# A two-layer decoder trunk on one core: the tensor engine's products of each attention issued in source order

## The chip, the cores and the metric

The kernel runs on one core of a Trainium2 chip. The metric is the device time of one execution in microseconds (us). The profile is that of one further execution; its span is the time between its first and its last recorded instruction.

## The reference, cut to what matters

256 tokens of width 1024 pass through two layers. The first attends with 16 heads of 64 to its own keys and values (at this length the block-sparse selection leaves the causal block of 256 alone); the second attends, in a sliding window of 128 with one learned sink per head, to four shared key and value heads. Each layer ends in a gated feed-forward part of width 2816 with a causal convolution of width 3.

```python
for l in range(DEPTH):                       # DEPTH = 2
    h = rmsnorm(x, attn_norm[l])
    if l < N_A:                              # layer 0
        q, k, v = jnp.split(h @ w_qkv_a[l], 3, axis=-1)
        o = moba_attention(rope(q), rope(k), v)
    else:                                    # layer 1, keys and values shared
        k, v = jnp.split(rmsnorm(x, kv_norm) @ w_kv_b, 2, axis=-1)
        o = swa_sink_attention(rope(h @ w_q_b[i]), rope(k), v, sinks_b[i])
    x = x + o @ w_o
    x = x + conv_ffn(rmsnorm(x, ffn_norm[l]), w_up[l], conv_w[l], conv_b[l], w_down[l])
return rmsnorm(x, final_norm)
```

## The kernel before, in words

All products keep float32 accuracy by splitting each operand into a rounded part ("hi") and the rest ("lo"); each product is three: hi with hi, hi with lo, lo with hi. The weights stream from memory in 90 units of 128 x 2048 (`wr`). For each, ScalarE (ACT) writes the hi part (`wh`, line 179) and VectorE (DVE) the lo part (`wl`, line 184), each in two or four pieces; both engines do this all through the program, a few units ahead of the TensorE (PE).

An attention (`attention`, line 408) works on four groups of four heads. For a group g:

- `scores(g)` (line 423): six products with the keys laid out in blocks (lines 432 to 434, into a bank `sd`), then twelve products that use half of the array's rows (line 439), two at a time, one for each of two banks `u`. Their operands are the queries and keys turned to feature order by `to_feature` (line 384): four transposes (line 388), a hi copy on ACT (line 399), a lo difference on DVE (line 394). The first four of the twelve need the hi part alone; the next two need the lo part.
- the softmax of each head (line 444): DVE masks the scores and takes their extreme (line 456), ACT takes the exponential (line 464), then DVE forms the reciprocal (line 469) and scales the first third of the row (line 476) while ACT scales the rest (line 474).
- `probs_T` (line 483): three transposes per head (line 489) into a bank `u`, of which the first reads what DVE scaled and the other two what ACT scaled; a copy out of the bank by DVE (line 497) or ACT (line 495).
- `values(g)` (line 503): eight products that use half of the array's columns (line 512; 16 entries in the profile), whose result is split into hi (ACT, line 518) and lo (DVE, line 519).

Between these pieces `fill` draws full-size products from a `filler`: projections of later heads (`proj`, lines 347 to 349), and then the output projection (`Down.mm`, lines 558 to 561; the hi products first, line 561 last, which needs the lo part of line 519). `attention` is called twice, for layer 0 (line 938) and layer 1 (line 1004).

What sets the order: steps on ACT and DVE are put off by a clock that the kernel keeps while it is written out (`chain`, `tick`), and the framework's scheduler then orders each engine's instructions by its own estimate of when each is ready. Inside `tc.manual_schedule(engines=...)` the engines named keep the order in which the source issues them. Before, this holds for PE, ACT, DVE and SP from the start to line 524 in layer 0 (`manual.close()`) and for ACT and DVE in the tail (line 1048); within the loop over the groups, PE's order is the scheduler's. In the trace each engine's instructions begin in the order in which they stand in the program, so that one that waits holds those behind it.

Of the kernel before, what the change touches and what calls it, by code (L numbers as in the profile page):

```python
# [60 lines left out]
def trunk(ctx: ExitStack, tc, x, xw, pos, cpk, fin, sinks, w, out):  # L61
# [20 lines left out]
    def quad(dt=F32R, name="q"):  # L82
        return spaced(qd, 4 * S, dt, "q", nm(name), 15).rearrange("p (c t) -> p c t", c=4)
# [4 lines left out]
    def row3(n=3 * P, edges=False):  # L88

        t = wk.tile([P, 3 * P + 8], F32, tag="m3", name=nm("m3"), bufs=8)  # L90
        return (t[:, 3:3 * P + 5], t[:, 4:3 * P + 4]) if edges else t[:, 4:4 + n]

    def bank(tag):
        return ps.tile([P, 512], F32, tag=tag, name=nm(tag), bufs=4 if tag == "acc" else 2)

    def f(ap):
        return ap.bitcast(F32)

    def blk(b):
        return slice(b * P, (b + 1) * P)  # L100
# [29 lines left out]
    def tick(ns):  # L130
        clock[0] += ns
        while put_off and not busy[0]:
            item = min(put_off, key=lambda t: t[0])
            if item[0] > clock[0]:
                return
            run_item(item)

    def chain(key, *steps, urgent=0):

        def run(k):  # L140
            if urgent:
                with tc.high_priority(offset=urgent):
                    steps[k][1]()
            else:
                steps[k][1]()
            if k + 1 < len(steps):
                put_off.append((clock[0] + steps[k + 1][0], key, lambda: run(k + 1)))
        put_off.append((clock[0] + steps[0][0], key, lambda: run(0)))

    def require(*key):  # L150

        while True:
            mine = [t for t in put_off if t[1] == key]
            if not mine:
                return
            run_item(min(mine, key=lambda t: t[0]))
# [251 lines left out]
    def attention(qk, ready, filler, lead, rate, msk, vcol, sink):  # L408
# [6 lines left out]
        def fill(ns):  # L415
            budget[0] += ns
            while budget[0] > 0:
                try:
                    budget[0] -= next(filler)
                except StopIteration:  # L420
                    return

        def scores(g):
            while g not in qk:
                next(filler)
            require("qk", g)
            qh, ql, kh_, kl_, kcol, diag = qk[g]
            sd, sa, sb = bank("t" if o_down[0].acc else "acc"), bank("u"), bank("u")
            for p in range(2):
                dh, dl = diag(p)  # L430
                o = sd[:, p * S:(p + 1) * S]
                nc.tensor.matmul(o, qh[:, p, blk(0)], dh, start=True, stop=False)
                nc.tensor.matmul(o, qh[:, p, blk(0)], dl, start=False, stop=False)
                nc.tensor.matmul(o, ql[:, p, blk(0)], dh, start=False, stop=True)
            for p in range(2):
                for k, (q_, k_) in enumerate(((qh, kh_), (qh, kl_), (ql, kh_))):
                    for e, o in enumerate((sa, sb)):
                        r = slice(e * HD, (e + 1) * HD)
                        nc.tensor.matmul(o[:, p * S:(p + 1) * S], q_[r, p, blk(1)], k_[r, kcol(p)],
                                         start=(k == 0), stop=(k == 2))  # L440
            tick(1600)
            return [softmax(2 * g + p, p, sd, (sa, sb)) for p in range(2)]
# [40 lines left out]
        def probs_T(j, pr):  # L483
            require("sm", j)
            out_ = []
            for e in range(2):
                tp = bank("u")
                for i in range(3):
                    nc.tensor.transpose(tp[:, i * P:(i + 1) * P], pr[e][:, i * P:(i + 1) * P], ident)  # L489
                tick(330)  # L490
                pT = row3()

                def copy(e=e, tp=tp, pT=pT):
                    if e:
                        nc.scalar.activation(pT, tp[:, :3 * P], AF.Copy)
                    else:
                        nc.vector.tensor_copy(pT, tp[:, :3 * P])

                chain(("pT", j), (200.0, copy))
                out_.append(pT)  # L500
            return out_

        def values(g, pT):

            ov = bank("t")
            for p in range(2):
                j = 2 * g + p
                require("pT", j)
                for kb in range(NB):
                    for e in range(2):  # L510
                        o = ov[e * HD:(e + 1) * HD, p * S:(p + 1) * S]
                        nc.tensor.matmul(o[:, P:] if kb else o, v_sb[kb][:, vcol(2 * j + e)],  # L512
                                         pT[p][e][:, S:] if kb else pT[p][e][:, :S], start=(kb == 0), stop=(kb == 1))
            tick(1600)
            q = quad()
            hi, lo = q[:, 0:2], q[:, 2:4]
            ov = ov.rearrange("p (j t) -> p j t", j=2)
            chain(("o", g), (200.0, lambda: nc.scalar.activation(hi, ov, AF.Copy)),
                  (600.0, lambda: nc.vector.tensor_tensor(out=lo, in0=ov, in1=f(hi), op=ALU.subtract)))
            oT.extend((hi[:, p], lo[:, p]) for p in range(2))  # L520
# [2 lines left out]
        fill(lead)  # L523
        manual.close()
        n_g = NH // 4
        state = scores(0)
        for g in range(n_g):
            pT = []
            for p in range(2):
                fill(rate(g)[p])  # L530
                pT.append(probs_T(2 * g + p, state[p]))
            fill(rate(g)[2])
            if g + 1 < n_g:
                state = scores(g + 1)
            values(g, pT)
        for _ in filler:
            pass
        return oT
# [396 lines left out]
    def ready_a(oT):  # L935
        o_down.append(Down(U_OA, 4, oT, lambda i: require("o", i)))

    attention(qk, ready_a, filler_a(), 8000.0, lambda g: (7000.0, 3500.0, 2000.0) if g < 3 else (4500.0, 2000.0, 1500.0), mask, lambda h: h, False)
    nc.gpsimd.affine_select(out=mask[:, :P], in_=mask[:, :P], compare_op=ALU.is_gt, fill=NEG, base=0,
                            pattern=[[1, P]], channel_multiplier=-1)  # L940
# [60 lines left out]
    def ready_b(oT):  # L1001
        o_down.append(Down(U_OB, 4, oT, lambda i: require("o", i)))

    attention(qk, ready_b, filler_b(), 2800.0, lambda g: (2700.0, 1400.0, 1000.0) if g else (3300.0, 1700.0, 1000.0), mask, lambda h: 2 * (h // 8) + h % 2, True)

    hT = new_hT()
# [149 lines left out]
```

## Time and profile before

| | us |
|---|---|
| median of 3 runs (lowest, highest) | 552.49 (552.43, 552.72) |
| the profiled execution | 551.98 |
| its span in the profile | 550.3 |
| PE busy | 542.5 |
| ACT busy | 372.8 |
| DVE busy | 419.9 |
| granted TensorE clock, mean | 0.998 |

1.7 us of the profiled execution lie around the span. "Busy" for PE is modelled: a product of 128 x 512 is shown with about 0.38 us, but the next one starts 0.22 us after it, so that the starts and not the durations tell what PE spends. The first attention's groups run from about 36 to 104 us of the span, the second's from about 316 to 360 us. In a row of the timeline stand the start, the time to the end of the last of the instructions merged in it, the engine, the source line, the operation, the output and inputs, the shape, and how many instructions are merged; in brackets the idle time ahead of it and what ended that.

### The profile page before, as it was taken

The page shows a single profiled execution, that of the slowest core. Times are in us where ns is not written, and L with a number is a line of the kernel's source. Part 1 is how long each engine was busy: PE and PEld are TensorE (multiplying, and loading weights), DVE is VectorE, ACT ScalarE, POOL GpSimd, SP SyncE. Part 2 cuts the span into 40 slices and gives each one's busy share as a digit, 9 for nine tenths or more (in the row PEclk, how much of TensorE's full clock was granted, in tenths as well). Part 3 has the DMA queues.
Part 4 walks back from the last instruction along what each step waited for, and adds up shares of the span by engine and source line. Part 5 has one row for each costly group of instructions (what it writes and reads, how often), then busy time and mean ns, then how long its engine had stood idle before and what let it go on. Part 6 is the DMA issues. An engine that isn't in the chain of part 4 may idle for free.

```text
span 550.3 us, 9930 instructions
## 1 busy us (share of the span) xinstructions
PE 542.5 (99%) x3762; PEld 497.7 (90%) x3762; DVE 419.9 (76%) x874; ACT 372.8 (68%) x726; POOL 113.3 (21%) x140
## 2 busy tenths in 40 slices
PE   8999999999999999999999999999999999999995
PEld 7888888899999999988888887889999999998884
DVE  6798778589798888865468789788898888884414
ACT  6998777678577777744448698877667777663313
POOL 7331001013322233220002000002532332210003
PEclk9999999999999999999999999999999999999999
DMA  8984335342555665565643524242465556665301
GB/s 322 384 302 166 142 153 191 116 155 78 200 212 205 227 230 206 186 232 219 208 174 154 198 109 154 78 152 77 154 249 211 210 195 213 248 224 215 114 0 76
DMA packets 15311, 100.98 MB, mean 184 GB/s; under 512 B 1952, under 2 KB 2080, under 8 KB 3744
## 3 DMA queue, kind: packets, MB, share of 16 engines
q1 hardware_dynamic: 14976, 100.09, 50.5%
q8 instruction: 29, 0.48, 0.3%
q10 hardware_dynamic: 288, 0.26, 0.1%
q14 instruction: 18, 0.15, 0.1%
HBM read 99.30 MB, written 1.05 MB: 182 GB/s over the span
## 4 chain that ended last, share of the span: by engine, by line
PE 97%; DMA 1%; issue 0%; POOL 0%; DVE 0%; DVEq 0%; POOLq 0%; ACT 0%
PE acc L558 10%; PE acc L559 9%; PE acc L561 9%; PE u L653 7%; PE u L651 7%; PE u L652 6%; PE t L653 6%; PE t L651 6%; PE t L652 6%; PE acc L347 5%; PE acc L349 5%; PE acc L348 5%; PE t L512 2%; PE u L489 2%; PE acc L765 2%; PE acc L653 2%
## 5 line engine op out<-in xcount | busy, mean ns | idle before, releaser
L184 DVE TENSOR_TENSOR wl<-wr,wh 128x1024 fp32r<-128x1024 f32 (+1 forms) x190 | 207.3, 1110 | 55.9 <-ACT wh L179 55.3
L179 ACT ACTIVATE wh<-wr 128x1024 fp32r<-128x1024 f32 (+1 forms) x190 | 176.4, 957 | 55.7 <-PE acc L561 44.6
L697 POOL TENSOR_TENSOR m<-m,m 128x256 f32<-128x256 f32 x44 | 70.6, 1605 | 166.7 <-DVE m L692 95.2
L558 PE MATMUL acc<-wh,q 128*128 128x512 f32 x238 | 92.1, 387 | 0.0
L559 PE MATMUL acc<-wl,q 128*128 128x512 f32 x238 | 90.9, 382 | 0.0
L651 PE MATMUL u<-q,wh 128*128 128x256 f32 x320 | 88.4, 277 | 0.0
L652 PE MATMUL u<-q,wh 128*128 128x256 f32 x320 | 88.1, 276 | 0.0
L653 PE MATMUL u<-q,wl 128*128 128x256 f32 x320 | 87.9, 275 | 0.0
L651 PE MATMUL t<-q,wh 128*128 128x256 f32 x288 | 79.2, 275 | 0.0
L653 PE MATMUL t<-q,wl 128*128 128x256 f32 x288 | 79.2, 275 | 0.0
L652 PE MATMUL t<-q,wh 128*128 128x256 f32 x288 | 79.2, 275 | 0.0
L561 PE MATMUL acc<-wh,q 128*128 128x512 f32 x238 | 74.7, 380 | 0.0
L653 PEld LDWEIGHTS u<-q,wl 128*128 128x128 f32 x320 | 61.4, 192 | 0.0
L652 PEld LDWEIGHTS u<-q,wh 128*128 128x128 f32 x320 | 61.4, 192 | 0.0
L651 PEld LDWEIGHTS u<-q,wh 128*128 128x128 f32 x320 | 61.3, 192 | 0.0
L652 PEld LDWEIGHTS t<-q,wh 128*128 128x128 f32 x288 | 55.3, 192 | 0.0
L653 PEld LDWEIGHTS t<-q,wl 128*128 128x128 f32 x288 | 55.3, 192 | 0.0
L651 PEld LDWEIGHTS t<-q,wh 128*128 128x128 f32 x288 | 55.3, 192 | 0.0
L558 PEld LDWEIGHTS acc<-wh,q 128*128 128x128 f32 x238 | 45.0, 189 | 6.9 <-issue 0.9
L561 PEld LDWEIGHTS acc<-wh,q 128*128 128x128 f32 x238 | 44.9, 189 | 6.3
L347 PE MATMUL acc<-wh,q 128*128 128x512 f32 x128 | 50.4, 394 | 0.0
L559 PEld LDWEIGHTS acc<-wl,q 128*128 128x128 f32 x238 | 45.0, 189 | 5.9 <-issue 0.2
(167 smaller groups left out, 995.8 us busy)
## 6 DMA issues: line engine op xcount, KB each, us to landing
wr<-in_w SPq DMA_DIRECT2D x90, 1024.0 KB, 4.8
first<-in_xw SPq DMA_DIRECT2D x5, 384.0 KB, 5.7
xr<-in_x SPq DMA_DIRECT2D x2, 512.0 KB, 8.2
first<-in_xw SPq DMA_DIRECT2D x1, 768.0 KB, 7.1
fin_t<-in_fin SPq DMA_DIRECT2D x1, 512.0 KB, 5.7
out<-ot SPq DMA_DIRECT2D x1, 512.0 KB, 2.6
first<-in_xw SPq DMA_DIRECT2D x1, 388.0 KB, 3.8
out<-m ACTq DMA_DIRECT2D x1, 256.0 KB, 2.1
```

Source lines behind the costliest of these rows:

```text
L179: nc.scalar.activation(wq[i][0][:, c], raws[i][:, c], AF.Copy, **({} if g is None else {"scale": g}))
L184: nc.vector.tensor_tensor(out=lo, in0=raw, in1=hi, op=ALU.subtract)
L347: nc.tensor.matmul(o, xh[:, blk(b)], wh, start=(c == 0), stop=False)
L348: nc.tensor.matmul(o, xh[:, blk(b)], wl, start=False, stop=False)
L349: nc.tensor.matmul(o, xl[:, blk(b)], wh, start=False, stop=(c == KC - 1))
L558: nc.tensor.matmul(o, ph[:, blk(b)], turns(hi[:, s_]), start=first, stop=False)
L559: nc.tensor.matmul(o, ph[:, blk(b)], turns(lo[:, s_]), start=False, stop=False)
L561: nc.tensor.matmul(o, pl[:, blk(b)], turns(hi[:, s_]), start=False, stop=end)
L651: nc.tensor.matmul(o, hi[:, s_], xh, start=(c == 0), stop=False)
L652: nc.tensor.matmul(o, hi[:, s_], xl, start=False, stop=False)
L653: nc.tensor.matmul(o, lo[:, s_], xh, start=False, stop=(c == KC - 1))
L697: nc.gpsimd.tensor_tensor(out=h, in0=gs, in1=t[1], op=ALU.mult)
```

## The change

The loop over the groups, from the first `scores(0)` to the last `values`, is put inside `tc.manual_schedule` for PE alone. ACT, DVE and the others stay with the scheduler there.

```diff
         manual.close()
         n_g = NH // 4
-        state = scores(0)
-        for g in range(n_g):
-            pT = []
-            for p in range(2):
-                fill(rate(g)[p])
-                pT.append(probs_T(2 * g + p, state[p]))
-            fill(rate(g)[2])
-            if g + 1 < n_g:
-                state = scores(g + 1)
-            values(g, pT)
+        with tc.manual_schedule(engines={mybir.EngineType.PE}):
+            state = scores(0)
+            for g in range(n_g):
+                pT = []
+                for p in range(2):
+                    fill(rate(g)[p])
+                    pT.append(probs_T(2 * g + p, state[p]))
+                fill(rate(g)[2])
+                if g + 1 < n_g:
+                    state = scores(g + 1)
+                values(g, pT)
         for _ in filler:
             pass
```

No instruction is added or taken away on any engine. In the first attention PE's order changes at one place, the scores of the last group; in the second it changes at a dozen places. The line numbers in the rows of the changed kernel are one higher from line 526 on. Numbers in the names of tiles count allocations, so the same tile has another number in the two kernels.

**First place: PE, scores of the last group of the first attention.** `t_1082` (then `t_1084`) is the bank of the six products with the keys in blocks, `u_...` the two banks of the twelve, `acc_...` the output projection. Before:

```order
L434 MATMUL t_1082<-kd_116,q_841 128x256
L558 MATMUL acc_1014<-wh_870,q_920 128x512
L559 MATMUL acc_1014<-wl_871,q_920 128x512
L439 MATMUL u_1083<-q_840 128x256
L439 MATMUL u_1084<-q_840 128x256
L558 MATMUL acc_1015<-wh_870,q_920 128x512
L559 MATMUL acc_1015<-wl_871,q_920 128x512
L561 MATMUL acc_1014<-wh_870,q_920 128x512
L561 MATMUL acc_1015<-wh_870,q_920 128x512
L558 MATMUL acc_1016<-wh_870,q_920 128x512
L559 MATMUL acc_1016<-wl_871,q_920 128x512
L439 MATMUL u_1083<-q_841,q_840 128x256
```

Changed:

```order
L434 MATMUL t_1084<-kd_116,q_843 128x256
L439 MATMUL u_1085<-q_842 128x256
L439 MATMUL u_1086<-q_842 128x256
L439 MATMUL u_1085<-q_843,q_842 128x256
L439 MATMUL u_1086<-q_843,q_842 128x256
L439 MATMUL u_1085<-q_842,q_843 128x256
L439 MATMUL u_1086<-q_842,q_843 128x256
```

Eight products of the output projection that stood in the two holes of the twelve now stand behind them and the eight of line 512.

**Second place: PE, the transposes of the first two heads in the second attention.** `m_338` and `m_339` are the two heads' softmax rows. Before:

```order
L489 MATMUL u_3741<-ident,m_338_3688 128x128
L489 MATMUL u_3753<-ident,m_339_3689 128x128
L347 MATMUL acc_3721<-wh_3504,q_1336 128x512
L489 MATMUL u_3741<-ident,m_338_3688 128x128 x2
L348 MATMUL acc_3721<-wl_3505,q_1336 128x512
L349 MATMUL acc_3721<-wh_3504,q_1337 128x512
L347 MATMUL acc_3721<-wh_3504,q_1336 128x512
L348 MATMUL acc_3721<-wl_3505,q_1336 128x512
L349 MATMUL acc_3721<-wh_3504,q_1337 128x512
L489 MATMUL u_3753<-ident,m_339_3689 128x128 x2
L347 MATMUL acc_3721<-wh_3552,q_1338 128x512
```

Changed:

```order
L489 MATMUL u_3746<-ident,m_338_3693 128x128 x3
L489 MATMUL u_3758<-ident,m_339_3694 128x128 x3
L347 MATMUL acc_3726<-wh_3507,q_1339 128x512
L348 MATMUL acc_3726<-wl_3508,q_1339 128x512
L349 MATMUL acc_3726<-wh_3507,q_1340 128x512
L347 MATMUL acc_3726<-wh_3507,q_1339 128x512
L348 MATMUL acc_3726<-wl_3508,q_1339 128x512
L349 MATMUL acc_3726<-wh_3507,q_1340 128x512
L347 MATMUL acc_3726<-wh_3555,q_1341 128x512
L348 MATMUL acc_3726<-wl_3556,q_1341 128x512
```

Six projection products that stood between the transposes now stand behind all six transposes. The same happens to the output projection's products at the first two heads of each later group of the second attention.

**Third place: DVE, ahead of the masking of the second group of the second attention.** `wl` is the lo part of a weight unit that is not needed until later, `q` the lo part of a query tile, `m_358` the first head's scores. Before:

```order
L497 COPY m_352_3784<-u_3775 128x384
L184 TENSOR_TENSOR wl_3773<-wr_3598,wh_3772 128x1024
L394 TENSOR_TENSOR q_3627<-t_3779,q_3626 128x4x128
L456 ISA m_358_3820,hst_3822<-acc_3798,mask,nsink 128x128
L456 ISA hst_3822 128x1
```

Changed:

```order
L497 COPY m_352_3789<-u_3780 128x384
L184 TENSOR_TENSOR wl_3778<-wr_3601,wh_3777 128x1024 x2
L394 TENSOR_TENSOR q_3630<-t_3784,q_3629 128x4x128
L456 ISA m_358_3825,hst_3827<-acc_3803,mask,nsink 128x128
L456 ISA hst_3827 128x1
```

The scheduler, which still orders DVE, now puts both halves of that weight unit ahead of the masking; before, the second half stood in the middle of the eight maskings (line 456). ACT's two halves of the same unit (line 179) likewise stand together now, ahead of the hi copy of line 399.

## Prediction

> **What bounds the kernel now.** Times without a unit are us. First the page's busy times, then its chain that ended last:
>
> ```profile
> PE 542.5 (99%) x3762; PEld 497.7 (90%) x3762; DVE 419.9 (76%) x874; ACT 372.8 (68%) x726; POOL 113.3 (21%) x140
> ...
> PE 97%; DMA 1%; issue 0%; POOL 0%; DVE 0%; DVEq 0%; POOLq 0%; ACT 0%
> ```
>
> PE is busy nearly throughout and makes up 97% of the chain. So every stretch in which PE stands still, or spends more than it must, is on the path, and behind the attentions nothing can take it back: there PE's order is the same in both kernels. The change touches nothing but PE's order in the attentions and, through the scheduler, a little of ACT's and DVE's. The question is thus what each reordered place costs PE. The waits view names almost no wait for PE there, so I went on to the timelines of PE, ACT and DVE, place by place.
>
> Two things can change. A scheduler that fills holes hides a wait; laid out in source order, PE stands at the waiting instruction. Against that, full products between half-array products cost extra at each seam, and those seams go.
>
> **(a) First attention, scores of the last group.** The timelines of PE, then ACT, then DVE:
>
> ```profile
> 89.58 0.38 PE L558 MATMUL acc<-wh,q 128*128 128x512 f32 x1
> ...
> 90.21 0.38 PE L439 MATMUL u<-q 64*128 64x256 f32 x2
> ...
> 91.06 0.59 PE L561 MATMUL acc<-wh,q 128*128 128x512 f32 x2
> 91.49 0.38 PE L558 MATMUL acc<-wh,q 128*128 128x512 f32 x1
> 91.71 0.38 PE L559 MATMUL acc<-wl,q 128*128 128x512 f32 x1
> 92.02 0.51 PE L439 MATMUL u<-q,q 64*128 64x256 f32 x4
> ...
> 92.80 1.52 PE L512 MATMUL t<-m,v 128*64 128x256 f32 x16
> 94.25 0.48 PE L558 MATMUL acc<-wh,q 128*128 128x512 f32 x1
> 94.57 0.38 PE L559 MATMUL acc<-wl,q 128*128 128x512 f32 x1
> ```
>
> ```profile
> 89.58 0.58 ACT L399 ACTIVATE q<-t 128x512 fp32r<-128x512 f32 x1
> ```
>
> ```profile
> 90.85 0.69 DVE L394 TENSOR_TENSOR q<-t,q 128x512 fp32r<-128x512 f32 x1
> ```
>
> A full product takes 0.216 (two from 91.06 to 91.49). The hi copy ends at 90.16 and PE's first pair begins at 90.21: 0.05 from an end to a waiting product. The lo part ends at 91.54. In the new order the first pair still begins at 90.21, but then PE stands until 91.59. From there everything is as it was from 92.02 to 94.25, 2.23, to 93.82. The eight full products that filled the holes (from 89.58 to 91.71) are still to be done: 8 x 0.216 = 1.73, to 95.55, where before stood at 94.25. **+1.30.** The cover that goes is those eight products; the lo part cannot be sooner, since the copies on ACT and DVE ahead of it stay in place.
>
> **(b, c) Second attention, first group.** DVE, PE, ACT:
>
> ```profile
> 316.81 0.69 DVE L394 TENSOR_TENSOR q<-t,q 128x512 fp32r<-128x512 f32 x1 [0.27 <-ACT q L399]
> ```
>
> ```profile
> 317.89 0.74 PE L439 MATMUL u<-q,q 64*128 64x256 f32 x8
> 318.56 0.48 PE L349 MATMUL acc<-wh,q 128*128 128x512 f32 x1
> ...
> 321.47 0.38 PE L489 MATMUL u<-ident,m 128*128 128x128 f32 x2
> ...
> 323.20 0.38 PE L489 MATMUL u<-ident,m 128*128 128x128 f32 x2
> 323.34 0.46 PE L347 MATMUL acc<-wh,q 128*128 128x512 f32 x1
> ```
>
> ```profile
> 322.42 0.49 ACT L474 ACTIVATE m<-m,hst 128x256 f32<-128x256 f32 x1
> ```
>
> (b) The lo part ends at 317.50, so the eight begin at 317.55 rather than 317.89 and end 0.67 later; two full products follow that before stood ahead of them. The third, at 318.56 before, comes at 318.76, but a seam is saved (0.32 rather than 0.22 for a product behind half-array ones, as from 94.25 to 94.57): **+0.1**.
>
> (c) The second head's last two transposes read what ACT scales from 322.42 to 322.91. Before, six full products lay ahead of them; now PE is at them at 322.1 and stands until 322.96. The two transposes and then the six products (0.15 + 0.30 + 5 x 0.216) bring it to the product of 323.34 at about 324.5: 1.1 late in all, **+1.0** for this place.
>
> **(d) Second group, first two heads.** DVE, ACT, PE:
>
> ```profile
> 327.70 0.34 DVE L456 CUSTOM_DVE_ANT_0 m<-acc,mask,nsink 128x128 f32<-128x128 f32 x1
> ...
> 329.04 1.22 DVE L184 TENSOR_TENSOR wl<-wr,wh 128x1024 fp32r<-128x1024 f32 x1
> ```
>
> ```profile
> 328.14 0.40 ACT L464 ACTIVATE m<-m,hst 128x129 f32<-128x129 f32 x1 [0.41 <-DVE hst L456]
> ...
> 330.77 0.69 ACT L980 ACTIVATE m<-acc,rstd 128x512 f32<-128x512 f32 x1 [0.29 <-PE acc L349]
> ...
> 333.18 1.30 ACT L474 ACTIVATE m<-m,hst 128x256 f32<-128x256 f32 x3
> ```
>
> ```profile
> 333.93 0.46 PE L558 MATMUL acc<-wh,q 128*128 128x512 f32 x1
> ...
> 334.36 0.46 PE L559 MATMUL acc<-wl,q 128*128 128x512 f32 x1
> ```
>
> The weight piece of 329.04 (1.2) now stands ahead of the first masking, and DVE's copy ahead of both comes some 0.2 later (an estimate: PE's delay of 1.1, less DVE's idle time there). The masking begins at 327.70 + 1.4 = 329.1, ACT's exponentials at 329.5. ACT took 5.04 from there to 333.18, 0.29 of it idle; without that idle it scales the first head at 329.5 + 4.75 = 334.3 and is done 0.5 later, 334.8. PE, 1.1 late, is at that transpose at about 333.1 and stands until 334.85. Then the remaining transposes (0.16 + 3 x 0.11 + 0.03), the six products that filled this hole before (0.30 + 5 x 0.216) and one more bring it to 336.9 for the product of 334.36: 2.5 late, **+1.4**, the largest term and the least certain one, since it hangs on a chain of fourteen instructions on ACT. Its bounds: if ACT's chain comes no later than before (333.18 + 0.5), the term is +0.3; if a weight piece of 1.2 more lies ahead, it is +2.6. I take +1.4, since DVE and ACT keep the new order whatever PE does.
>
> **(e to h) Third and fourth group.** PE, then ACT:
>
> ```profile
> 339.21 0.73 PE L439 MATMUL u<-q,q 64*128 64x256 f32 x8
> ...
> 341.33 0.48 PE L559 MATMUL acc<-wl,q 128*128 128x512 f32 x1
> ...
> 345.83 0.38 PE L558 MATMUL acc<-wh,q 128*128 128x512 f32 x1
> ...
> 348.24 0.86 PE L512 MATMUL t<-m,v 128*64 128x256 f32 x6
> 349.03 0.97 PE L439 MATMUL u<-q,q 64*128 64x256 f32 x12
> 349.93 1.08 PE L512 MATMUL t<-m,v 128*64 128x128 f32 x10
> 350.94 0.48 PE L558 MATMUL acc<-wh,q 128*128 128x512 f32 x1
> ...
> 357.72 0.87 PE L512 MATMUL t<-m,v 128*64 128x256 f32 x8
> ...
> 359.95 0.48 PE L558 MATMUL acc<-wh,q 128*128 128x512 f32 x1
> ```
>
> ```profile
> 344.13 1.69 ACT L474 ACTIVATE m<-m,hst 128x256 f32<-128x256 f32 x4
> ...
> 353.76 1.70 ACT L474 ACTIVATE m<-m,hst 128x256 f32<-128x256 f32 x4
> ```
>
> (e) As in (b), the pair that needs the lo part waits, now behind one masking on DVE: five full products, ten transposes (0.11 each) and the six with the keys in blocks (0.12 each) bring PE from 336.9 to 339.8, their result is there at 340.1, the masking (0.3) and the difference (0.7, as in (b)) end at 341.1, so the eight begin at 341.2 instead of 339.21. From there to the product of 341.33 it is 2.12, and three full products are still to be done: 343.95, 2.6 late, **+0.1**. Two holes' seams pay for the wait.
>
> (f) The scores are 1.97 late, so the scaling of 344.13 ends at 346.1 + 0.5. PE is at that transpose at 346.1, stands 0.5, and with the order turned comes to the product of 345.83 about 3.05 late (three small products that stood ahead counted): **+0.45**.
>
> (g) The eight of line 512 in one piece take 1.45 (92.80 to 94.25); cut by the twelve they took 0.79 + 1.01. And from 357.72 to 359.95 two pieces with two full products between took 2.23, where 1.45 + 2 x 0.216 is enough. **-0.35 each.** (h) The scaling of 353.76, 2.25 late with its scores, ends at 356.5, and PE, 2.7 late, is there at 356.45: **+0.1**.
>
> **Sum:** 1.30 + 0.10 + 1.0 + 1.4 + 0.1 + 0.45 - 0.7 + 0.1 = 3.75 on the profiled execution's 551.98 (span 550.3 and 1.7 around it), 555.7. That execution lies 0.5 below the median of the runs shown, 552.49; on the median it is **556.2**.
>
> **Rivals.**
>
> *The seams win; faster.* By (g) a cut through half-array products costs about 0.35. With (g)'s two the order shows some seven that go: 2.5 off, 550.0. It needs the lo parts and ACT's scaled rows to be there when PE comes. The point that decides is the lo part of (a): it would have to end by 90.4, and it ends at 91.54. 0.03.
>
> *The waits of the second attention are repaid.* Terms (c), (d) and (f) are not independent: a late PE lets ACT and DVE catch up, so each later wait shrinks. Taken to the end, only (a) is left, since behind it the first attention has no moved product: 553.8. Against it speaks that the scores feed ACT, so a late PE makes ACT late too. 0.07.
>
> *The delays feed each other.* ACT and DVE are the bound in the second attention, and each of them lays a weight piece ahead of the softmax. Two further waits like (d)'s give 2.8 more: 559.0. ACT's idle of 0.41 and 0.29 in the rows of (d) speaks against it. 0.08.
>
> *PE's clock drops.* In the tail, PE's last piece of the chain stands in the first row, and the second is the windows view there, the clock granted ahead of its last two columns:
>
> ```profile
> 541.11 0.23 PE acc L561
> ```
>
> ```profile
> 538.00:550.30 12.30, 5.96 (x34) 5.21 (x32) 5.62 (x16) 4.71 (x12) 4.91 (x5) 0.92 0.22 85
> ```
>
> The mean of 0.92 over 12.3 means half speed from about 548.3, some 7 after the last product. If a wait did that once and it lasted as long, it would add 3.4: 559.6. My longest wait is 1.7, and PE works on both sides of it. 0.02. [...]
>
> That the change doesn't do what it says is excluded by the rows of the order shown.
>
> **How the numbers follow.** The forecast, slower by about 3.7, has 0.80. Its own spread is that of (d), 1.1 down and 1.2 up, and some 0.5 for the rest: 554.6 to 557.9. I widen it to 554.2 to 558.4; seams, full repayment and the two dearer cases, 0.20 together, lie outside. 0.2%, about what a measurement of this kernel can tell from no change, is 1.1: slower by over 0.2% begins at 553.6. Faster 0.03, within 0.2% 0.04 (half of the repaid case, which lies at that border), slower 0.93.
>
> **What would show it.** PE's timeline of the changed kernel should show the twelve of line 439 in one piece everywhere; in the first attention a stop of 1.1 to 1.4 after the first pair, ended by DVE's line 394; in the second attention stops ended by ACT's line 474, of about 0.9 in the first group, over 1 in the second, about 0.5 in the third. PE's work at the end of the first attention should be 1.3 later than before, at the end of the second about 3.7. It would be wrong if ACT's and DVE's rows move up when PE's order changes, so that the stops are short, or if the stops come at other instructions.

## The result and the profile after

| | before | changed |
|---|---|---|
| median of 5 runs, us (lowest, highest) | 552.49 (552.41, 552.72) | 557.20 (556.59, 558.56) |
| ratio, 95% interval | | 1.0083 (1.0071 to 1.0095) |
| profiled execution, us; its span | 551.98; 550.3 | 556.77; 555.1 |
| granted TensorE clock, mean over the span | 0.998 | 0.998 |

The changed kernel is slower by about 4.7 us, 0.8%. Two more series of it gave 1.0094 (1.0079 to 1.0109) and 1.0086 (1.0072 to 1.0101). Executions that were disturbed as a whole are left out of the figures below, and so is the trace of the seventh experiment, which is of such a one.

The page of the changed kernel, busy times and the chain that ended last:

```profile
PE 542.4 (98%) x3762; PEld 498.3 (90%) x3762; DVE 420.1 (76%) x874; ACT 372.9 (67%) x726; POOL 114.9 (21%) x140
...
PE 87%; ACT 4%; DMA 3%; DVE 3%; issue 1%; POOL 1%; DVEq 0%; POOLq 0%; ACTq 0%
```

PE does the same work in the same busy time, but the chain now leaves PE, in the attentions for ACT and DVE. The DMA's 3% lie at the start, ahead of 27 us (two transfers of 6.61 and 8.84), which the chain reaches through a stop at 30 us spoken of below. The windows view shows where PE stops in the attentions: the stretch, its length, the busy time of PE, PE's weight loads, DVE, ACT and POOL with their counts, the clock, the DMA share. First the two stretches before, then after:

```profile
88.00:104.00 16.00, 15.96 (x108) 12.64 (x107) 10.69 (x34) 11.88 (x31) 0.29 (x1) 1.00 0.42 146
...
316.00:370.00 54.00, 53.99 (x354) 43.32 (x353) 45.09 (x153) 46.60 (x133) 2.79 (x12) 1.00 0.37 129
```

```profile
88.00:104.00 16.00, 14.53 (x96) 11.94 (x96) 10.93 (x35) 11.35 (x30) 0.29 (x1) 1.00 0.38 132
...
316.00:370.00 54.00, 50.59 (x331) 40.67 (x329) 42.33 (x140) 42.96 (x119) 3.37 (x12) 1.00 0.34 118
```

PE was idle for 0.04 and 0.01 there and now is for 1.47 and 3.41. The waits view of the changed kernel (who waits for whom: us in total, times, the longest) names the causes:

```profile
PE u L489 <- ACT m L474: 2.5, 4, 1.2
PE u L439 <- DVE q L394: 1.9, 3, 1.0
...
PE u L439 <- ACT q L399: 0.5, 1, 0.5
PE t L388 <- DVE m L382: 0.4, 1, 0.4
```

The first three come to 4.9; with some 0.7 of seams saved that leaves 4.2. The last row lies at 30 us, ahead of the first moved product, and is looked at below. The stops in PE's timeline, first attention and then the four groups of the second:

```profile
90.83 0.38 PE L439 MATMUL u<-q 64*128 64x256 f32 x2 [0.48 <-ACT q L399]
92.20 0.50 PE L439 MATMUL u<-q,q 64*128 64x256 f32 x4 [0.99 <-DVE q L394]
...
96.48 0.38 PE L560 MATMUL acc<-wl,q 128*128 128x512 f32 x1
```

```profile
324.81 0.44 PE L489 MATMUL u<-ident,m 128*128 128x128 f32 x2 [0.72 <-ACT m L474]
...
336.54 0.84 PE L489 MATMUL u<-ident,m 128*128 128x128 f32 x5 [1.21 <-ACT m L474]
...
348.36 0.84 PE L489 MATMUL u<-ident,m 128*128 128x128 f32 x5 [0.35 <-ACT m L474]
...
358.84 0.84 PE L489 MATMUL u<-ident,m 128*128 128x128 f32 x5 [0.23 <-ACT m L474]
...
365.06 0.38 PE L560 MATMUL acc<-wl,q 128*128 128x512 f32 x1
```

The product of 96.48 stood at 94.57 before: 1.9 late. That of 365.06 stood here:

```profile
360.27 0.38 PE L559 MATMUL acc<-wl,q 128*128 128x512 f32 x1
```

It is 4.79 late, as much as the two profiled executions differ, so nothing behind the attentions takes it back. Of this 0.61 was there ahead of the first moved product; 4.18 came with the places. The shift of the same product between two traces, read in this way at each place, is the measure used from here on ("shift").

### The profile page after: what moved, and what is told of

It reads as the page before. It is cut to its first block, busy times and chain, and to the rows that moved or that the text cites. A ratio compares the mean times of both kernels' runs of the same rounds, so it can differ in the third digit from the quotient of the medians.

```text
span 555.1 us, 9927 instructions
## 1 busy us (share of the span) xinstructions
PE 542.4 (98%) x3762; PEld 498.3 (90%) x3762; DVE 420.1 (76%) x874; ACT 372.9 (67%) x726; POOL 114.9 (21%) x140
## 4 chain that ended last, share of the span: by engine, by line
PE 87%; ACT 4%; DMA 3%; DVE 3%; issue 1%; POOL 1%; DVEq 0%; POOLq 0%; ACTq 0%
PE acc L559 9%; PE acc L560 9%; PE acc L562 9%; PE u L652 6%; PE u L654 6%; PE u L653 6%; PE t L652 6%; PE t L654 6%; PE t L653 6%; PE acc L347 4%; PE acc L349 4%; PE acc L348 4%; DMA wr<-in_w 3%; PE acc L652 2%; PE acc L654 2%; PE acc L653 2%
## 5 line engine op out<-in xcount | busy, mean ns | idle before, releaser
L698 POOL TENSOR_TENSOR m<-m,m 128x256 f32<-128x256 f32 x44 | 73.1, 1663 | 164.1 <-DVE m L693 94.0
```

Of the source, the lines that this page charges most:

```text
L698: nc.gpsimd.tensor_tensor(out=h, in0=gs, in1=t[1], op=ALU.mult)
```

## The experiments

Each edit is against the changed kernel unless said otherwise. `manual(...)` stands for `tc.manual_schedule(engines={...})`.

**1 and 2. One attention alone.**

```diff
-        with manual(PE):
+        with ExitStack() if sink else manual(PE):     # 1: first attention alone
+        with manual(PE) if sink else ExitStack():     # 2: second attention alone
```

> The source order for PE in the first attention alone. Theory (each place costs its own wait, and places add): +1.3 by the end of the first attention's moved products, second attention as before: 553.8. Rival 1 (the start-up delay of 0.6 seen at 30 us comes with the edit itself, through the order of the weights' transfers): 554.4, with the 0.6 there at 30 us. Rival 2 (delays of the first attention make the second's waits): over 554.5.

> The source order for PE in the second attention alone. Theory: the sum of the second attention's places, 2.9: 555.4, with PE stopped at the same instructions as in the changed kernel. Rival 1 (the 0.6 at the start comes with the edit): 556.0. Rival 2 (the second attention's waits come from PE being 1.3 late out of the first): below 554.5.

Measured: the first, 553.22 in the profiled execution and 555.27 to 555.61 in four more; ratio 1.0055 (1.0042 to 1.0068). The second, 555.06 to 555.63; 1.0052 (1.0039 to 1.0065). In the profiles the first attention alone shifts PE by 1.30, the second alone by 2.86 from 38 us on, which makes 4.16; the changed kernel has 4.18. The waits of the second alone are, row for row, those of the second attention in the changed kernel:

```profile
PE u L489 <- ACT m L474: 2.5, 4, 1.2
...
PE u L439 <- DVE q L394: 0.9, 2, 0.7
```

So the places add, and neither attention makes the other's waits. The shifts at 30 us were -0.08 and 0.2, against the 0.6 of the changed kernel: that delay doesn't come with the edit. No theory foresaw the four executions of the first that were 2 longer than its profile.

**3. Cover put back at the scores.**

```diff
+            fill(hole(g))                      # ahead of the twelve of line 439
             for p in range(2):
                 for k, (q_, k_) in enumerate(((qh, kh_), (qh, kl_), (ql, kh_))):
```

with a hole of six products in the first attention's last group and of three and six in the second's first and third, and as many taken from the fills behind.

> The changed kernel, with full products put by hand between the products with the keys in blocks and the twelve half-array ones at the three places where PE stopped there (six in the last group of the first attention, three in the first and six in the third group of the second), and as many fewer behind. Theory (there the cost is the lost cover): L394's and L399's waits go, -1.2 in the first attention, -0.1 to -0.4 in the second: 555.5 to 556.0. Rival (what is saved at the scores is waited for again at the transposes, since ACT and DVE are late): 556.8 to 557.3, with L474's waits longer than 2.5 in all.

Measured: 554.27 to 554.97, ratio 1.0040 (1.0028 to 1.0052), below what the theory gave. In the first attention the shift is 0.03 at most instead of 1.30, so the whole of that term was lost cover. The second attention has 2.31 instead of 2.88, a gain of 0.57 where at most 0.4 was expected. The hole of the first group made it: that group, up to the values, costs 0.25 instead of 0.88. The second group then costs 1.68 instead of 1.49, and the hole of the third group gave little (0.42 for its scores and transposes together, instead of 0.58). There PE's stop moved (line numbers here are one, behind 526 two higher):

```profile
344.95 0.48 PE L560 MATMUL acc<-wh,q 128*128 128x512 f32 x1 [1.38 <-ACT q L519]
```

The six products drawn forward into the scores of the third group had been the cover for the hi part of the second group's values (line 518), and PE now waits for that. The same six products did not cover both waits.

**4. The transposes later.**

```diff
-lambda g: (2700.0, 1400.0, 1000.0) if g else (3300.0, 1700.0, 1000.0)
+lambda g: (4000.0, 100.0, 1000.0) if g else (4600.0, 400.0, 1000.0)
```

> The changed kernel, with six full products in each group of the second attention moved from between the first and the second pair of heads' transposes to ahead of the first pair's. Theory (the transposes come too soon, and nothing else is short): L474's waits of 2.5 in all go, and some 0.4 of lost cover with them: 554.3 to 554.8. Rival (ACT and DVE are the bound in the second attention, the wait only moves to the second pair's transposes or to the scores): 556.0 to 557.3.

Measured: 553.89 to 554.52 in four executions, 556.34 to 557.78 in three; ratio 1.0054 (1.0032 to 1.0076). No wait at L474 is left. The second group, +1.50 in the changed kernel, became -0.4, the third -0.1, the fourth about 0. In the first group the rival held. PE, then ACT:

```profile
327.37 0.55 PE L489 MATMUL u<-ident,m 128*128 128x128 f32 x3 [1.28 <-ACT m L495]
```

```profile
325.04 0.95 ACT L474 ACTIVATE m<-m,hst 128x256 f32<-128x256 f32 x2
325.90 1.04 ACT L179 ACTIVATE wh<-wr 128x1024 fp32r<-128x1024 f32 x1
326.85 0.47 ACT L495 ACTIVATE m<-u 128x384 f32<-128x384 f32 x1
```

The second pair's transposes came only three products behind the first pair's and waited for a bank that ACT frees with its copy, behind a weight piece of 1.04. The edit did more than move PE's products: the scheduler changed ACT's order with them, and the first scaled row of the second group stands at 333.62, where the changed kernel has it at 335.98.

**5. DVE in source order too, in the second attention.**

```diff
-        with manual(PE):
+        with manual(PE, DVE) if sink else manual(PE):
```

> The changed kernel, with DVE too in source order through the second attention's groups; PE's order is the same as in the changed kernel. In the second group the second half of the weight piece (L184) then stands behind the first eight maskings, as it does before the change; in the third group a weight piece now stands ahead of them. Theory (the second group's 1.5 comes from that weight piece ahead of the softmax): the wait there falls from 1.2 to at most 0.4 and PE's shift over that group from 1.5 to 0.3 to 0.6, while the third group's wait grows by up to 1.2 from 0.35. Rival (PE's own order alone is to blame, the transposes come six products too soon): both waits within 0.2 of the changed kernel's, time 557.

Measured: 558.37 to 560.06, ratio 1.0122 (1.0106 to 1.0138). The second group's shift fell from 1.50 to 1.20 only. ACT's scaled rows of that group in the changed kernel, and here, and PE here:

```profile
335.98 1.30 ACT L474 ACTIVATE m<-m,hst 128x256 f32<-128x256 f32 x3
```

```profile
336.04 1.29 ACT L474 ACTIVATE m<-m,hst 128x256 f32<-128x256 f32 x3
```

```profile
335.27 0.70 PE L562 MATMUL acc<-wh,q 128*128 128x512 f32 x2 [0.54 <-DVE q L519]
...
336.59 0.84 PE L489 MATMUL u<-ident,m 128*128 128x128 f32 x5 [0.51 <-ACT m L474]
```

With the weight piece behind the first eight maskings the scaled rows come at the same time; measured from the group's scores, which are 0.35 later here, they gain 0.3. So the theory fails for that group. PE's wait of 1.2 is cut in two, since line 519 now comes later. In the third group a weight piece ahead of the softmax did what the expectation says, and something more. PE's timeline, and the windows with the granted clock in the column ahead of the last two:

```profile
349.48 0.84 PE L489 MATMUL u<-ident,m 128*128 128x128 f32 x5 [1.71 <-ACT m L474]
350.07 0.65 PE L559 MATMUL acc<-wh,q 128*128 128x512 f32 x1
350.51 0.63 PE L560 MATMUL acc<-wl,q 128*128 128x512 f32 x1
350.94 0.63 PE L559 MATMUL acc<-wh,q 128*128 128x512 f32 x1
...
353.79 0.38 PE L560 MATMUL acc<-wl,q 128*128 128x512 f32 x1
```

```profile
350.00:351.00 1.00, 1.00 (x6) 0.82 (x6) 0.96 (x4) 1.00 (x2) 0.37 (x2) 0.61 0.00 0
351.00:352.00 1.00, 1.00 (x4) 0.82 (x3) 1.00 (x1) 0.95 (x3) 0.00 (x0) 0.50 0.00 0
352.00:353.00 1.00, 1.00 (x4) 0.80 (x3) 0.04 (x1) 0.00 (x0) 0.00 (x0) 0.50 0.00 0
353.00:354.00 1.00, 1.00 (x4) 0.79 (x3) 0.00 (x0) 0.00 (x0) 0.00 (x0) 0.68 0.00 0
```

Behind the stop of 1.71 the products start 0.43 apart instead of 0.216, at a clock of 0.50. By the four rows that costs 0.39 + 0.50 + 0.50 + 0.32 = 1.7, so the clock was at half for some 3.4 us.

**6. Source order from the second group on.** The kernel before, with PE in source order only there, and the later transposes of experiment 4:

```diff
         for g in range(n_g):
+            with manual(PE) if sink and g else ExitStack():
...
+lambda g: (4000.0, 100.0, 1000.0) if g else (3300.0, 1700.0, 1000.0)
```

> The kernel before, with PE in source order only from the second group of the second attention on, and there with six products more ahead of the first pair of heads' transposes. Theory (PE's source order costs only what its waits cost, and saves seams): no wait of PE at L474 over 0.3, the first attention and the first group as before, 0.3 to 1.0 below before: 551.4 to 552.1. Rival 1 (ACT and DVE are the bound there whatever PE's order): waits of 1 and more come back at the second pair's transposes or the copies, 553 to 554. Rival 2 (executions some 2 longer are disturbances that any kernel has): some of them here too.

Measured: 552.90 to 553.98 in twelve executions, ratio 1.0014 (1.0006 to 1.0023). Of the shift of 1.50 at the end 0.50 was there ahead of the second attention. The other 1.00 came at the waits of PE:

```profile
332.77 0.70 PE L562 MATMUL acc<-wh,q 128*128 128x512 f32 x2 [0.67 <-DVE q L519]
...
337.63 0.55 PE L489 MATMUL u<-ident,m 128*128 128x128 f32 x3 [0.36 <-ACT m L495]
...
343.78 0.48 PE L559 MATMUL acc<-wh,q 128*128 128x512 f32 x1 [0.40 <-ACT q L518]
```

The first rival held, in small: the softmax is waited for no more, but three other results of ACT and DVE are.

**7 and 12. Experiment 1 again, twice. 8 and 11. The changed kernel again, twice.**

> The kernel of the first experiment once more (source order in the first attention alone). There the profiled execution took 553.2, as the places give, but the others some 555.4, with a mean granted clock of 0.994 in three of four where it is 0.996 to 0.999 elsewhere. Theory (PE's two stops in the first attention, 0.5 and 1.0 within 2 us, in some executions make the granted clock fall for a few us behind them): half or more of the executions near 555.4 again, and in a profile of one of them full products 0.43 apart instead of 0.22 for some 4 us within 8 us behind the stops. Rival (a delay at the start or a disturbance from outside): the loss lies elsewhere, or the executions come out near 553.2.

> The changed kernel once more, unaltered. Theory (places cost 4.2 in all; the 0.6 at the start is a scatter of that one execution): 556.2 to 556.8 for the executions without a fall of the clock, and in the profile a shift at 30 us between -0.1 and 0.6, the places as before within 0.1. With the theory of the clock's fall, some executions 1.5 to 2.2 longer, at 558 to 559. Rival (the 0.6 at 30 us belongs to the edit): 0.5 to 0.7 there again.

> The changed kernel a third time, unaltered. Theory (places 4.2, start 0 to 0.7, and in some executions a fall of the clock worth 1.6 to 2 behind a stop of PE): executions between 556.2 and 557.6, and about one in three near 558.6 with a mean clock of 0.993 to 0.995; a profile of one of those shows full products 0.43 apart for some 3.3 us right behind one of the stops. Rival (the longer executions come from outside the attentions): a longer execution's profile shows all products behind the stops 0.22 apart and its loss at the start or elsewhere.

> The kernel of the first experiment (source order in the first attention alone) a third time, unaltered, as the first two series of it differ in median (555.43 and 553.94). Theory (fall of the clock in some executions): two groups of executions, 553.2 to 554.2 with a clock of 0.996 to 0.998 and near 555.5 with 0.993 to 0.995, about one in three in the second; a profile of the second kind shows full products 0.43 apart for some 3.3 us within 8 us behind the two stops. Rival (the longer executions come from the start): a longer execution's profile shows the loss ahead of 36 us.

Measured: 7, nine executions from 553.33 to 554.21 with a mean clock of 0.996 to 0.998 and two at 555.79 and 555.83 with 0.994. 12, two at 554.30 and 554.45 (0.998, 0.997), three from 555.26 to 555.80 (0.994). 8, 556.87 to 558.79, of which two with 0.995 and 0.994 (557.82, 558.79), but also one of 558.56 with 0.997. 11, 556.42 to 556.85 and one of 558.06 with 0.995. Ratios: 7, 1.0030 (1.0019 to 1.0041); 12, 1.0052 (1.0039 to 1.0065). None of these traces is of an execution with a low clock. The shifts at the places agree in the three traces of the changed kernel: 4.18 to 4.19 from 38 us on. At 30 us they were 0.6, 0.7 and 0.25; in experiment 12, 1.1. A part of that is there by 12 us (0.01, -0.27, 0.25 and 0.18). The rest comes between 29 and 30 us: 0.57, 0.94, 0 and 0.92. There PE's transposes wait for DVE and ACT, and these for a weight transfer, which the trace of before happens to have in time. The rows of before, of the changed kernel, and of experiment 12:

```profile
23.04 3.44 ACT L179 ACTIVATE wh<-wr 128x512 fp32r<-128x512 f32 x6
```

```profile
26.14 1.15 ACT L179 ACTIVATE wh<-wr 128x512 fp32r<-128x512 f32 x2 [0.80 <-DMA wr<-in_w]
```

```profile
26.67 1.15 ACT L179 ACTIVATE wh<-wr 128x512 fp32r<-128x512 f32 x2 [1.67 <-DMA wr<-in_w]
```

In the two with the stop that are shown, PE's next full product starts 4.28 behind that piece of ACT (26.14 to 30.42 and 26.67 to 30.95). The changed kernel has the stop in two of its three traces, the kernel of experiments 1 and 12 in one of two. So it scatters from execution to execution and is no effect of the change.

**9. A longer stop.** Experiment 1 with the twelve of line 439 ahead of the six of lines 432 to 434 in the first attention's last group (`blocks` and `halves` are the two loops, made functions):

```diff
+            for part in (halves, blocks) if not sink and g == 3 else (blocks, halves):
+                part()
```

> The kernel of the first experiment (source order in the first attention alone), with the twelve half-array products of its last group ahead of the six products with the keys in blocks, so that PE stops sooner: about 1.2 for the hi part and then 1.0 for the lo part, within some 2.5 us. By the places: the first attention +1.3 and the six products of 0.12 that no longer cover the wait, +2.0 in all, 554.4. Theory (stops that fill a good part of a few us let the granted clock fall to half for some 3.3 us, as behind the stop of 1.7 in the fifth experiment): most executions lose 1.5 to 1.9 more, 556 to 556.4 with a clock of 0.994, and the profile shows full products 0.43 apart behind 92 us. Rival (the clock falls only behind an unbroken stop of over 1.5, and the longer executions of the first experiment had another cause): about 554.4, clock 0.996 to 0.999, all products 0.22 apart.

Measured: 554.48, 554.69, 555.47, 556.33 and 556.36, all with a clock of 0.996; ratio 1.0059 (1.0045 to 1.0072). The stops are as foreseen:

```profile
90.91 0.39 PE L442 MATMUL u<-q 64*128 64x256 f32 x2 [1.20 <-ACT q L399]
92.29 0.51 PE L442 MATMUL u<-q,q 64*128 64x256 f32 x4 [0.99 <-DVE q L394]
```

The shift is 2.2 for the 2.0 forecast. The profiled execution (554.69) shows no fall of the clock behind them (1.00 in each window of 1 us from 90 to 100). Two executions 1.8 longer, without a lower mean clock, leave the question where it was: a longer stop does not make the fall certain.

**10. One seam alone.** The kernel before, with PE in source order only in these lines:

```diff
+            with manual(PE) if sink and g > 1 else ExitStack():
                 if g + 1 < n_g:
                     state = scores(g + 1)
                 values(g, pT)
```

> The kernel before, with PE in source order only through the scores of the second attention's last group and the values of its last two groups, so that the eight half-array products of the values (L512), cut in two before by the twelve of the scores, stand in one piece behind them; the order of the rest of PE is the scheduler's. Theory (a cut through those products costs 0.35, as the seam term of the prediction has it): PE's shift over that place -0.2 to -0.35 and no new wait, 552.1 on a median before of 552.4. Rival (the cut is free, or the lo part or a bank is waited for in its place): a shift of 0 or more.

Measured: 551.97 to 553.13, ratio 1.0000 (0.9991 to 1.0009). PE at this place:

```profile
350.03 1.52 PE L512 MATMUL t<-m,v 128*64 128x256 f32 x16
...
352.61 0.48 PE L559 MATMUL acc<-wh,q 128*128 128x512 f32 x1 [0.21 <-ACT q L518]
```

The eight in one piece bring the shift from 0.20 to -0.21 at the first product behind them and to -0.11 from the next one on: the seam is worth 0.3. Then PE waits for ACT's line 518, and is at 0.29 by the end. The seam is real, and here it is given back within 1 us.

## Why the prediction was right, and where it was off

Place by place, the shift that each adds in the changed kernel:

| place | predicted | measured |
|---|---|---|
| (a) first attention, scores of the last group | 1.30 | 1.30 |
| (b) second attention, scores of the first group | 0.10 | 0.11 |
| (c) its first pair's transposes | 1.0 | 0.94 |
| scores of the second group: a gap of before that closes | - | -0.17 |
| (d) second group's transposes | 1.4 | 1.50 |
| (e) scores of the third group | 0.1 | 0.08 |
| (f) third group's transposes | 0.45 | 0.50 |
| (g) two seams | -0.70 | -0.71 |
| (h) fourth group's transposes | 0.1 | 0.64 |
| sum | 3.75 | 4.19 |

The steps held: PE stops at the instructions named, for the engines named, and nothing behind the attentions takes it back. The stops have the sizes forecast, if they are counted from where the usual spacing of starts would have put the next instruction (the idle time in brackets is shorter, since it counts from a modelled end): 1.25 for 1.1 to 1.4 in the first attention, and 0.88, 1.43 and 0.51 for 0.9, over 1 and 0.5 in the second. The stop of 0.48 ahead of the first pair is in the prediction's working, but not in its list of signs. Of its rivals, neither repayment nor delays that feed each other came: the second attention costs 2.88 where the sum has 2.45, and no second wait is as long as (d)'s. Experiments 1 and 2 show that the terms add; 3 shows that (a) is lost cover and nothing else; in 4, where six products more stand ahead of the transposes, (d), (f) and (h) go.

**(h) was mis-sized**, by 0.54, where the whole sum is off by 0.44. Two waits make it up. The first: the prediction let the scaled rows be as late as line 439's products, 2.25. DVE and ACT of the changed kernel:

```profile
353.31 0.35 DVE L456 CUSTOM_DVE_ANT_0 m<-t,mask,nsink 128x128 f32<-128x128 f32 x1 [0.59 <-PE t L434]
```

```profile
358.30 1.69 ACT L474 ACTIVATE m<-m,hst 128x256 f32<-128x256 f32 x4
```

The scaling is 4.54 later than the 353.76 of before, and without the start (0.61) and (a) it is 2.63 later, not 2.25. The masking begins with the six products with the keys in blocks, not with line 439. Before, three of those six stood 5.6 us ahead of the rest:

```profile
342.32 0.29 PE L434 MATMUL t<-kd,q 128*128 128x256 f32 x1
...
348.02 0.29 PE L434 MATMUL t<-kd,q 128*128 128x256 f32 x1
```

In source order all six stand together, behind the transposes, and DVE waits for the last one. PE came about when it was forecast, so the 0.4 became its wait (from the 358.44 that the spacing of transposes gives to the 358.84 of the row). The second was not foreseen: ahead of these transposes PE's weight load (PEld) waits for ACT's line 518, the hi part of the third group's values, as PE did in experiment 10 at this place. That takes PE's shift from 4.50 to 4.70:

```profile
356.93 0.19 PEld L559 LDWEIGHTS acc<-wh,q 128*128 128x128 f32 x1 [0.33 <-ACT q L518]
```

**(d) had the right size with a reason that fell.** The prediction laid the late row to the weight piece that goes ahead of the masking on DVE. The steps came as forecast: without the 1.91 of the start and (a), the masking begins 1.29 late (1.4 forecast), and ACT takes 4.64 from its first exponential to the row (4.75 forecast). But experiment 5 puts that piece back behind the first eight maskings, and the row gains 0.3, no more: ACT then takes 5.42, with stops of 0.37 and 0.18 for DVE. The row is as late as the group's scores are, by (c): 2.80 against 2.79. So it was partly luck that the size fitted.

When PE comes decides the rest. In experiment 6 the row lies against the scores as it does here (both 0.50 late), and PE, behind six products more and the stop at line 519, comes when it is there. ACT's row, then PE's transposes, without a stop:

```profile
333.68 1.29 ACT L474 ACTIVATE m<-m,hst 128x256 f32<-128x256 f32 x3
```

```profile
334.60 0.82 PE L489 MATMUL u<-ident,m 128*128 128x128 f32 x6
```

In experiment 4 the term goes too, but there the row comes 2.36 sooner as well (333.62), so it doesn't show which of the two did it.

**The clock.** The prediction gave a fall of the clock 0.02, on the ground that no stop lasts 7 as in the tail. The 7 was misread: the row at 541.11 is the last of PE in the chain, but PE's last product before the change lies at 543.69 to 543.97, and the clock there, 1.00 up to 548.4, is 0.50 from 548.6 on, some 4.5 behind it (3.9 in the changed kernel, from 548.76 to about 552.7). Experiment 5 shows a fall behind a stop of 1.71, at a price of 1.7; no run shows the 3.4 of that rival. Stops of 1.28 and 1.38 in the traces of experiments 4 and 3 are followed by none (the full products behind them start 0.21 to 0.22 apart). Whether the first attention's two stops of 0.48 and 0.99 do it too is not seen in a trace. For it speaks the mean clock: in the kernels with these two stops as the change makes them (the changed kernel, experiments 1, 4, 7, 8, 11, 12) 15 of 44 executions have 0.995 or less; in the kernel before, run beside them, and in experiments 2, 3, 6 and 10, none of 90. (Experiment 5 has these stops too, but also a fall of its own, and is left out.) In experiments 7 and 12 the median of those executions is 1.9 and 1.3 above that of the others; a mean lower by 0.003 over 553 is 1.7 of lost clock. Against it speaks experiment 9, with longer stops and no clock of 0.995 or less in five. So the cause of these executions stays open. What sets the clock the runs do not show either: in experiment 5 PE stood still for 1.71 ahead of the fall and worked on both sides of it, in the tail it stood still for some 4.5 and had no work left.

**What the median holds.** 4.2 of the 4.7 are the places. The rest fits scatter that the trace of before didn't show: the start (-0.1 to 1.1 in these traces; 0.61 in the profiled execution) and, in some executions, the longer ones above. The third series, 556.56 on a before of 552.36, has 4.2.

## What to carry to other kernels

A scheduler that fills holes with full products can hide waits that the waits view of its profile hardly names, as here those that came to 4.9 us; before an order is fixed by hand, look at each product that reads another engine's result, how far ahead of its need that result was, and what stood in between. To size a wait in a new order, take the shift of the instruction that really feeds it (here the six products with the keys in blocks, not the twelve behind them). A product moved to cover one wait uncovers another: of the three attempts here to have the source order without its waits, each lost part of its gain to a result further down.

## What the runs showed that was not expected

- The granted clock fell to half for some 3.4 us behind a single stop of PE of 1.71, with PE at work on both sides (0.61, 0.50, 0.50 and 0.68 in four windows of 1 us); a stop of 1.38 in another trace was followed by none.
- A weight transfer at the start landed at a different time in three traces (before, the changed kernel, experiment 12): ACT waited 0, 0.80 and 1.67 for it, and PE's work behind it moved by 0, 0.57 and 0.92. So here single executions of two kernels compare to about 1 us, unless shifts are read from behind that point.
